# A sum of two weight blocks formed by an accumulating transfer instead of VectorE, in a hybrid encoder block

## The chip, the core and the metric

The kernel runs on one core of a Trainium2 chip. The core's engines work side by side, each through its own list of instructions in order: TensorE (PE) multiplies matrices, VectorE (DVE) and ScalarE (ACT) work element by element on tiles of 128 partitions, GpSimd (POOL) does a little arithmetic and issues transfers, and SyncE (SP) issues transfers only. Transfers between main memory and the core's on-chip memory (SBUF) are carried out by 16 DMA engines, whichever engine issued them. The metric is the device time of one execution, in microseconds; the time before is the median of three runs.

## What is computed

One residual layer over 512 tokens of 2048 features, in float32. Cut to what the change touches:

```python
proj = u @ W_in                        # u = RMSNorm(h); q, k, v, conv_a, conv_b, gates ga and gb
m    = sigmoid(ga) * y_A + sigmoid(gb) * y_B
h    = h + RMSNorm(m @ W_out)
u    = RMSNorm(h)
gate, up = split(u @ W_gate_up)        # 2048 x (2 * 5632)
h    = h + RMSNorm((silu(gate) * up) @ W_down)
```

The two products of the change are those of the gates (two times 2048 output features) and of the FFN's gate and up (two times 5632). All other parts (attention, convolution, output and down projection) keep their code.

## The kernel before

**Layout.** Activations are kept as [feature, token], so weights are the stationary operand and 512 tokens the moving one. A float32 operand is split into a high part (hi, made by a cast on ScalarE, L218 and L124) and a low part (lo, the difference, made on VectorE, L220 and L125); a product is three matmuls, hi by lo, hi by hi and lo by hi (L223 to L225).

**Stages in order.** Convolution inputs, v, q and k with attention, gates, LayerNorm and output projections, FFN gate and up, FFN down projection. The gates' tiles 0 and 1 and the FFN's tiles 0 to 4 run as plain products while the operands of the rest are made. The rest goes in pairs of output tiles through `strassen` (L195): pairs g2 to g15 in the loop at L526 (14 pairs, one tile of ga with one of gb) and pairs f5 to f43 in the loop at L708 (39 pairs, one tile of gate with one of up).

**One pair.** The pair's weights are four quarters of 128 x 1024 float32, 512 KB each: A11 and A12 are the halves of the first tile's rows of weights, A21 and A22 those of the second's. `quarter` (L203) loads each one on SP's queue into a buffer of the pool `wp`, tag `raw`, of which there are six, shared with all other weight loads. `wsum` (L208) makes a sum or difference of two such tiles on VectorE into the pool `stp`, tag `S`, three buffers:

```python
s1 = wsum(a21, a22, ALU.add, 1)
s2 = wsum(s1, a11, ALU.subtract, 2)
s3 = wsum(a11, a21, ALU.subtract, 3)
s4 = wsum(a12, s2, ALU.subtract, 4)
```

`product` (L216) splits one of these weight tiles (three buffers each for hi and lo) and multiplies it by one prepared block of the activations, in 24 matmuls of 128 x 128 by 128 x 256. There are seven products to a pair, in the order A11, S2, S1, S3, A12, S4, A22. A21 has no product of its own. The results go to PSUM tiles x, y and z; VectorE and ScalarE form sums of them in tiles of tag `quad` (L232, L236, L240, L243, L244). Behind each pair the gates' loop applies a sigmoid and stores the result by ScalarE's queue (ga at L531 to L534, gb at L535 to L538), and the FFN's loop forms silu(gate) * up and stores it (L715 to L721).

**What sets the order.** The program is written pair by pair, but the order in which an engine sees its instructions is set by a scheduler, which moves the preparation of the next pair (loads, casts, sums) into the current one as far as buffers allow. The order is then fixed, and each engine waits in it for its next instruction's inputs and buffers. A few loads are pinned to their place in the program (`load_in_order`, L85).

**Other buffers.** The pool `sp` has 69 slots of 128 x 512 float32 (`slot`). In the gates' stage it holds 64 tiles of prepared activation blocks, the column sum of the convolution (csum) and the tiles of ga and gb; in the FFN's stage it holds 56 operand tiles beside those of the results. The down projection reads the FFN's results back from main memory by GpSimd's queue (`load`, tile ad, L705).

Of the kernel before, what the change touches and what calls it, by code (L numbers as in the profile page):

```python
"""Bidirectional hybrid encoder block on one Trainium2 core.

Everything is kept feature-major ([feature, token]), so that a projection is
weights (stationary) times activations (moving, 512 tokens) and the output of
one projection is the moving operand of the next. Tokens are in the order
(column block of 16, grid row, column in block), so that a query block needs
only its own and its neighbouring blocks of keys.

float32 products: each operand is split exactly into hi (12 significant bits)
and lo (the rest, 12 bits), and hi*hi + hi*lo + lo*hi is accumulated in float32.  # L10

Gates and FFN gate/up (but for a few tiles that run while the operands are made)
take one step of Strassen-Winograd on top: their moving operand is RMS-normalized
by token, so that sums of its blocks keep float32's accuracy for every token.
"""
# [10 lines left out]
F32 = mybir.dt.float32  # L26
F32R = mybir.dt.float32r
AF = mybir.ActivationFunctionType
ALU = mybir.AluOpType
AX = mybir.AxisListType  # L30

P = 128
# [17 lines left out]
# where the next part's operands are prepared, in tiles; taps of the convolution per chunk of weights  # L50
# [12 lines left out]
def hybrid_block(ctx: ExitStack, tc, xT, vecs, rpb, mask, w_c0, w_qk, w_v, w_cg, w_ao, w_co, w_out, w_g0, w_gu, w_dn, outT):  # L63
    nc = tc.nc
    PSUM = bass.MemoryType.PSUM
    const = ctx.enter_context(tc.tile_pool(name="const", bufs=1))
    wp = ctx.enter_context(tc.tile_pool(name="wp", bufs=3))
    sp = ctx.enter_context(tc.tile_pool(name="sp", bufs=69))
# [16 lines left out]
    def load_in_order(out, src):  # L85
        """a load behind the loads above it, so that it takes no buffer long before its use"""
        tc.keep_in_program_order(nc.sync.dma_start(out, src))
# [13 lines left out]
    # TensorE's clock is up before the first products  # L101
# [4 lines left out]
    behind = [nc.scalar, nc.tensor]  # L106

    def follow(eng, ins):
        """pins the first instruction of an engine behind what was issued to it before the loads arrive"""
        if eng in behind:  # L110
            behind.remove(eng)
            tc.keep_in_program_order(ins)
# [16 lines left out]
    def split(src, name, scale=None):  # L129
        """src * scale (by partition) as hi + lo"""  # L130
        hi = slot(f"{name}h", F32R)
        lo = slot(f"{name}l", F32R)
        if scale is None:
            nc.scalar.copy(hi, src)
            nc.vector.tensor_tensor(out=lo, in0=src, in1=hi.bitcast(F32), op=ALU.subtract)
        else:
            follow(nc.scalar, nc.scalar.activation(hi, src, AF.Copy, scale=scale))
            nc.vector.scalar_tensor_tensor(
                out=lo, in0=src, scalar=scale, in1=hi.bitcast(F32), op0=ALU.mult, op1=ALU.subtract
            )  # L140
        return hi, lo

    def gemm(outs, acts, name, n=None, more=None, cols=slice(0, NT), between=(), pin=False):
        """ps[128 features, 512 tokens] = src[128, K/128 * 128].T @ acts for each (ps, src) of outs"""
        n = n or len(acts)
        between = iter(between)
        for c in range(0, n, 8):
            w = min(8, n - c)
            while len(acts) < c + w:
                acts.append(more(len(acts)))  # L150
            for i, (ps, src) in enumerate(outs):
                hi, lo = wchunk(src[:, c * P : (c + w) * P], f"{name}_{i}_{c}")
                for k in range(w):
                    s = slice(k * P, (k + 1) * P)
                    ah, al = (t[:, cols] for t in acts[c + k])
                    first, last = c + k == 0, c + k == n - 1
                    mmul = nc.tensor.matmul(ps, hi[:, s], al, start=first, stop=False)  # L157
                    if pin and k == 0:
                        tc.keep_in_program_order(mmul)
                    nc.tensor.matmul(ps, hi[:, s], ah, start=False, stop=False)  # L160
                    nc.tensor.matmul(ps, lo[:, s], ah, start=False, stop=last)  # L161
                next(between, lambda: None)()

    def interleaved(ps, hi, lo, acts, c, cols=slice(0, NT)):
        """the products of two tiles of features (2c, 2c + 1), with the weights for each of the four outputs ps"""
        for k in range(2):
            ah, al = (t[:, cols] for t in acts[2 * c + k])
            for n, o in enumerate(ps):
                o, s = o[:, cols], slice((k * 4 + n) * P, (k * 4 + n + 1) * P)
                first, last = c + k == 0 and cols.start == 0, 2 * c + k == KT - 1  # L170
                follow(
                    nc.tensor, nc.tensor.matmul(o, hi[:, s], ah, start=first, stop=False, skip_group_check=True)
                )
                nc.tensor.matmul(o, lo[:, s], ah, start=False, stop=False, skip_group_check=True)
                nc.tensor.matmul(o, hi[:, s], al, start=False, stop=last, skip_group_check=True)

    def winograd_t(u1, u2, t12, t34):
        """[T1 | T2] and [T3 | T4] of the block columns u1 = [B11 | B12] and u2 = [B21 | B22] (T4 negated)"""
# [16 lines left out]
    def strassen(w0, w1, op, name, n):  # L195
        """
        [w0; w1] (weights of two tiles of outputs, each [128, 2048]) times [B11 B12; B21 B22] by one step of
        Strassen-Winograd: 7 products of half the features by half the tokens in place of 8.
        Returns (C11, P1, C12 = z + u2, C21 = y + P1, C22): C11, z, y in PSUM, the others in SBUF.
        """  # L200
# [25 lines left out]

        a11, a21, a22, a12 = quarter(w0, 0), quarter(w1, 0), quarter(w1, 1), quarter(w0, 1)
        product(x, a11, "11", first=True)
        s1 = wsum(a21, a22, ALU.add, 1)
# [5 lines left out]
        u2 = quad(2)  # L235
# [9 lines left out]
        s4 = wsum(a12, s2, ALU.subtract, 4)  # L245
# [4 lines left out]
    def rstd(acc, n, name, blocks=range(NB), pin=False):  # L250
        """
        1/sqrt(mean + eps) by token (of the given blocks) from tiles [feature, token] whose sum by column
        is that of the squares: [token, block]
        """
# [15 lines left out]
    def by_column(r, name, blocks=range(NB), pin=False):  # L270
        """r [token, block] as a row on all partitions, in PSUM"""
# [14 lines left out]
    def halves(row, acc, name, n, pin=False):  # L286
        """the two steps to 1/rms for half n of the tokens, to row"""
        blocks, cols = range(n * NB // 2, (n + 1) * NB // 2), (A, B)[n]
        r = []
# [5 lines left out]
    def sumsq(acc, x, name, last=False, eng=nc.vector):  # L295
        """acc, a list of tiles, with x*x added (the last one as a tile of its own)"""
# [13 lines left out]
    # x * gain is split; 1/rms, a factor by token, is applied to what is projected from it.  # L310
# [32 lines left out]
    def taps(n):  # L343
        """the next n taps of the convolution, behind what VectorE does for the products"""
# [37 lines left out]
    def normalize(c):  # L382
        """tiles 2c and 2c + 1 of u = RMSNorm_pre(x), split"""
# [218 lines left out]
    # the last two by halves of the tokens, so that 1/rms of the first half is there when the products end  # L602
# [17 lines left out]
    # Gate and up for the first three tiles of the FFN, from h2 * gain: the 1/rms of h2 is applied to the result.  # L620
# [3 lines left out]
    def h2(i, cols):  # L624
        """h2 = x + f * gain / rms(f) into f[i], and its split, for some of the tokens"""
# [36 lines left out]
    # The next two from the normalized u, whose blocks (half of the features, half of the tokens) are kept:  # L662
    # B11 and B12 as [hi | lo] by block, B21 and B22 as hi and lo over all tokens.
# [36 lines left out]
    # The rest by Strassen-Winograd.  # L700
# [46 lines left out]
    # The last two tiles by halves of the tokens, so that the first half is finished beside the second's products.  # L747
# [53 lines left out]
def _mask():  # L801
    """0 where a key column lies in a query column's window, else a number that exp sends to 0"""
# [12 lines left out]
def _layout(x, mix_pre_g, mix_post_g, w_in, rpb, w_attn_o, w_dw, b_dw, conv_ln_g, conv_ln_b, w_conv_o, w_out,  # L815
# [16 lines left out]
    # bias of a query (row r, column c of its block) with a key (row, column of the block before, its own, the next)  # L832
# [5 lines left out]
    # gate and up columns of tiles 0 and 1, 3 and 4 of the FFN, by row of 128  # L838
    gu = w_gate_up[0].reshape(KT // 2, 2, P, 2, FT, P)[:, :, :, :, (0, 1, 3, 4)].reshape(KT // 2, 2, P, 2, 2, 2, P)
    gu = gu.transpose(4, 0, 2, 1, 5, 3, 6).reshape(2, KT // 2, P, 8 * P)  # L840
    # columns a and b of tiles 0 and 1 of the convolution, by row of 128
# [38 lines left out]
```

## Time and profile before

| | us |
|---|---|
| median of three runs | 2603.82 (2601.86 to 2605.2) |
| span of the profiled execution | 2602.3 |
| TensorE busy | 2561.6 |
| VectorE busy | 1748.0 |
| ScalarE busy | 975.4 |
| GpSimd busy | 187.5 |

The profile's page gives no time of its own for the profiled execution beside its span, so the span is taken for it. "Busy" counts the time in which an engine works on an instruction; waiting, and the issuing of transfers, are not in it. A row of the timeline has the start, the duration, the engine, the source line, the operation, the output and the inputs with their shapes, and in brackets how long the engine had been idle and what ended that. Names are those of the tiles, without their running numbers: f18s is any of the sums of pair f18, f18q any of its quarters, f18h and f18l a hi and a lo, f18v a `quad` tile; tiles named g belong to the gates. A releaser such as "PE f L224" names an engine, its output and its line.

### The profile page before, as it was taken

How to read it: one execution, taken by the hardware profiler on the slowest of the kernel's cores; microseconds unless marked ns; L12 is line 12 of the kernel's file. 1: busy time of each engine (PE TensorE's matmuls, PEld its weight loads, DVE VectorE, ACT ScalarE, POOL GpSimd, SP SyncE). 2: the span in 40 equal slices, each digit the busy share in tenths (PEclk: the TensorE clock that was granted, in tenths of full speed). 3: DMA queues.
4: the chain of work that ended last, by engine and by line, in shares of the span. 5: the costliest groups of instructions: out<-in, count | busy, mean ns of one | idle time of the engine just before them, and what ended most of it. 6: DMA issues, size and time to landing. Idle time of an engine off the chain costs nothing.

```text
span 2602.3 us, 38788 instructions
## 1 busy us (share of the span) xinstructions
PE 2561.6 (98%) x15950; PEld 2317.7 (89%) x15950; DVE 1748.0 (67%) x2178; ACT 975.4 (37%) x1351; POOL 187.5 (7%) x207
## 2 busy tenths in 40 slices
PE   9999999999999999998999999999999999999996
PEld 8888888899998888887899999999999988887886
DVE  5999895787775564348988777777777742233336
ACT  5223333444444322224444444444444432233222
POOL 0110222000000020004000000000000010010003
PEclk9999999999999999999999999999999999999998
DMA  6244323233336345233333333333333453353334
GB/s 214 93 130 149 108 93 105 93 130 136 133 122 219 126 146 174 97 119 141 110 118 110 118 126 121 112 117 122 123 119 118 149 197 99 97 170 95 94 92 141
DMA packets 109410, 330.18 MB, mean 127 GB/s; under 512 B 12592, under 2 KB 19888, under 8 KB 109232
## 3 DMA queue, kind: packets, MB, share of 16 engines
q1 hardware_dynamic: 88832, 283.68, 32.6%
q10 hardware_dynamic: 14976, 26.19, 2.7%
q0 software_dynamic: 5424, 17.83, 2.0%
q8 instruction: 125, 2.05, 0.3%
q14 instruction: 53, 0.43, 0.1%
HBM read 295.14 MB, written 32.51 MB: 126 GB/s over the span
## 4 chain that ended last, share of the span: by engine, by line
PE 81%; issue 15%; DVE 3%; DMA 1%; ACT 0%; POOL 0%; DVEq 0%; POOLq 0%; ACTq 0%
PE f L224 10%; PE f L223 10%; PE f L225 10%; PE pd L157 6%; PE pd L160 6%; PE pd L161 5%; PE po L157 2%; PE po L160 2%; PE po L161 2%; PE qk L161 2%; PE qk L160 2%; PE qk L157 2%; PE py L161 2%; PE py L160 2%; PE py L157 2%
## 5 line engine op out<-in xcount | busy, mean ns | idle before, releaser
L125 DVE TENSOR_TENSOR wlo_wd<-raw_wd,whi_wd 128x1024 fp32r<-128x1024 f32 (+1 forms) x90 | 102.3, 1136 | 279.8 <-ACT whi_wd L124 279.4
L124 ACT CAST whi_wd<-raw_wd 128x1024 fp32r<-128x1024 f32 (+1 forms) x90 | 88.4, 982 | 306.8 <-PE pd L160 305.7
L349 DVE SCALAR_TENSOR_TENSOR cv<-z,vec,cv 128x497 f32<-128x497 f32 (+14 forms) x240 | 190.8, 796 | 4.7
L125 DVE TENSOR_TENSOR wlo_wo<-raw_wo,whi_wo 128x1024 fp32r<-128x1024 f32 x36 | 47.5, 1318 | 106.9 <-ACT whi_wo L124 106.9
L705 POOL DMA_DIRECT2D ad<-a_d x44 | 23.7, 541 | 1020.9 <-DVE f36s L210 668.1
L124 ACT CAST whi_wo<-raw_wo 128x1024 fp32r<-128x1024 f32 x36 | 37.9, 1053 | 130.0 <-PE po L160 122.7
L124 ACT CAST whi_y<-raw_y 128x1024 fp32r<-128x1024 f32 x32 | 33.4, 1051 | 81.8 <-PE py L160 74.5
L124 ACT CAST whi_qk<-raw_qk 128x1024 fp32r<-128x1024 f32 x32 | 33.6, 1051 | 77.2 <-PE qk L160 48.0
L125 DVE TENSOR_TENSOR wlo_qk<-raw_qk,whi_qk 128x1024 fp32r<-128x1024 f32 x32 | 40.6, 1269 | 32.0 <-ACT whi_qk L124 31.7
L125 DVE TENSOR_TENSOR wlo_y<-raw_y,whi_y 128x1024 fp32r<-128x1024 f32 x32 | 53.3, 1667 | 10.0 <-ACT whi_y L124 9.8
L578 DVE TENSOR_TENSOR gg<-py,gg 128x512 f32<-128x512 f32 x32 | 22.0, 690 | 55.2 <-PE py L161 55.0
L157 PE MATMUL py<-ycl,whi_y 128*128 128x512 f32 x128 | 49.8, 389 | 0.0
L160 PE MATMUL py<-ych,whi_y 128*128 128x512 f32 x128 | 49.8, 389 | 0.0
L161 PE MATMUL py<-ych,wlo_y 128*128 128x512 f32 x128 | 49.8, 389 | 0.0
L428 POOL TENSOR_TENSOR bm<-braw,msk 128x128 f32<-128x128 f32 x56 | 43.7, 814 | 13.2 <-DMA braw<-in_rpb 13.2
L267 POOL TENSOR_TENSOR r_r<-r_v,mhalf 128x2 f32<-128x2 f32 (+1 forms) x6 | 8.6, 1436 | 465.5 <-DVE r_v L265 465.5
L125 DVE TENSOR_TENSOR wlo_f<-raw_f,whi_f 128x1024 fp32r<-128x1024 f32 x20 | 26.4, 1326 | 6.6 <-ACT whi_f L124 6.6
L457 ACT ACTIVATE sc<-sc,st 128x256 f32<-128x256 f32 (+1 forms) x32 | 18.0, 563 | 33.0 <-DVE st L456 32.0
L124 ACT CAST whi_ca<-raw_ca 128x1024 fp32r<-128x1024 f32 x12 | 12.6, 1053 | 47.2 <-PE cb L160 19.0
L588 POOL TENSOR_TENSOR gg<-gg,gg 128x512 f32<-128x512 f32 x16 | 20.6, 1288 | 113.8 <-ACT whi_y L124 76.5
L157 PEld LDWEIGHTS py<-ycl,whi_y 128*128 128x128 f32 x128 | 24.0, 188 | 5.0
L160 PEld LDWEIGHTS py<-ych,whi_y 128*128 128x128 f32 x128 | 24.0, 188 | 5.0
(11200 smaller groups left out, 10207.1 us busy)
## 6 DMA issues: line engine op xcount, KB each, us to landing
raw_wd<-in_w_dn SPq DMA_DIRECT2D x60, 512.0 KB, 3.5
raw_wo<-in_w_out SPq DMA_DIRECT2D x36, 512.0 KB, 3.6
raw_qk<-in_w_qk SPq DMA_DIRECT2D x32, 512.0 KB, 3.6
raw_wd<-in_w_dn SPq DMA_DIRECT2D x30, 384.0 KB, 3.1
a_d<-sg ACTq DMA_DIRECT2D x44, 256.0 KB, 2.0
ad<-a_d POOLq DMA_DIRECT2D x44, 256.0 KB, 5.0
raw_v<-in_w_v SPq DMA_DIRECT2D x16, 512.0 KB, 4.2
raw_y<-in_w_ao SPq DMA_DIRECT2D x16, 512.0 KB, 3.6
```

What stands on the lines that cost most here:

```text
L124: nc.scalar.copy(hi[:, s], raw[:, s])
L125: nc.vector.tensor_tensor(out=lo[:, s], in0=raw[:, s], in1=hi[:, s].bitcast(F32), op=ALU.subtract)
L157: mmul = nc.tensor.matmul(ps, hi[:, s], al, start=first, stop=False)
L160: nc.tensor.matmul(ps, hi[:, s], ah, start=False, stop=False)
L161: nc.tensor.matmul(ps, lo[:, s], ah, start=False, stop=last)
L223: nc.tensor.matmul(ps, hi[:, s], al, start=first and k == 0, stop=False, skip_group_check=True)
L224: nc.tensor.matmul(ps, hi[:, s], ah, start=False, stop=False, skip_group_check=True)
L225: nc.tensor.matmul(ps, lo[:, s], ah, start=False, stop=last and k == HT - 1, skip_group_check=True)
L349: nc.vector.scalar_tensor_tensor(out=a[:, to], in0=z[:, fr], scalar=col(C_WDW, i * CW + w), in1=a[:, to], op0=ALU.mult, op1=ALU.add)
L428: nc.gpsimd.tensor_tensor(out=bm[:, o + i - i0], in0=raw[:, :, i * BC : (i + 1) * BC], in1=msk[:, o + i - i0, None, :].broadcast_to([P, RO ...
L578: nc.vector.tensor_tensor(out=g, in0=ps, in1=g, op=ALU.mult)
L705: nc.gpsimd.dma_start(t, a_d[k])
```

## The change

In each pair the sum S1 = A21 + A22 is formed in a tile of its own, tag `S1` of the pool `stp`, with two buffers: SP loads A21 into it, and GpSimd then issues a transfer of A22 that adds to what is there. VectorE's addition is left out. A21 and A22 are still loaded as quarters too, for S3 and for the seventh product. S4 is written over S2 in S2's tile. The pool `sp` has 66 slots in place of 69. The rest of the diff blanks comments and docstrings; behind the new lines (L228 to L230), lines are numbered 3 higher than before within `strassen` (L243 is L246) and 4 higher after it (L535 is L539).

```diff
-    sp = ctx.enter_context(tc.tile_pool(name="sp", bufs=69))
+    sp = ctx.enter_context(tc.tile_pool(name="sp", bufs=66))
...
+        s1 = stp.tile([P, 1024], F32, tag="S1", name=f"{name}s1", bufs=2)
+        nc.sync.dma_start(s1, w1[:, :1024])
+        nc.gpsimd.dma_start(s1, w1[:, 1024:], accum_op=ALU.add)
         a11, a21, a22, a12 = quarter(w0, 0), quarter(w1, 0), quarter(w1, 1), quarter(w0, 1)
         product(x, a11, "11", first=True)
-        s1 = wsum(a21, a22, ALU.add, 1)
         s2 = wsum(s1, a11, ALU.subtract, 2)
...
-        s4 = wsum(a12, s2, ALU.subtract, 4)
+        s4 = s2
+        nc.vector.tensor_tensor(out=s4, in0=a12, in1=s2, op=ALU.subtract)
         product(z, s4, "22", last=True)
         product(y, a22, "T4", last=True)
```

The first place is VectorE's list within pair f18, before the change (here a tile's name has its number: s1 to s4 are the sums, v the `quad` tiles, q a quarter, h and l a hi and a lo):

```order
L220 TENSOR_TENSOR f18l_14566<-f18s1_14530,f18h_14564 128x1024
L210 TENSOR_TENSOR f18s4_14657<-f18q_14500,f18s2_14532 128x1024
L210 TENSOR_TENSOR f19s1_14763<-f19q_14729,f19q_14731 128x1024
L220 TENSOR_TENSOR f18l_14598<-f18s3_14594,f18h_14596 128x1024
L236 TENSOR_TENSOR f18v2_14592<-f18_1_14492,f18v1_14534 128x256
L210 TENSOR_TENSOR f19s2_14765<-f19s1_14763,f19q_14727 128x1024
L220 TENSOR_TENSOR f18l_14628<-f18q_14500,f18h_14626 128x1024
L220 TENSOR_TENSOR f18l_14661<-f18s4_14657,f18h_14659 128x1024
L210 TENSOR_TENSOR f19s3_14827<-f19q_14727,f19q_14729 128x1024
L243 TENSOR_TENSOR f18v4_14654<-f18_1_14492,f18v1_14534 128x256
L244 TENSOR_TENSOR f18v4_14654<-f18v4_14654,f18v3_14624 128x256
L220 TENSOR_TENSOR f18l_14689<-f18q_14498,f18h_14687 128x1024
```

S1 and S2 of pair f19 are made in pair f18. The same list of the changed kernel, from S4 of pair f18 to the lo of A22, the last row:

```order
L249 TENSOR_TENSOR f18s2_14533<-f18q_14503,f18s2_14533 128x1024
L722 TENSOR_TENSOR su17_14483<-f17_1_14259,f17v1_14302 128x256
L220 TENSOR_TENSOR f18l_14567<-f18s1_14494,f18h_14565 128x1024
L723 TENSOR_TENSOR sg17_14482<-sg17_14482,su17_14483 128x256
L220 TENSOR_TENSOR f18l_14599<-f18s3_14595,f18h_14597 128x1024
L239 TENSOR_TENSOR f18v2_14593<-f18_1_14492,f18v1_14535 128x256
L210 TENSOR_TENSOR f19s3_14828<-f19q_14730,f19q_14732 128x1024
L220 TENSOR_TENSOR f18l_14629<-f18q_14503,f18h_14627 128x1024
L220 TENSOR_TENSOR f18l_14661<-f18s2_14533,f18h_14659 128x1024
L210 TENSOR_TENSOR f20s2_14999<-f20s1_14960,f20q_14963 128x1024
L246 TENSOR_TENSOR f18v4_14655<-f18_1_14492,f18v1_14535 128x256
L220 TENSOR_TENSOR f18l_14689<-f18q_14501,f18h_14687 128x1024
```

No sum S1 is left, S4 of f18 stands ahead of the lo of its S1, and the S2 that is made within pair f18 is now that of f20, two pairs on, which reads the tile that the transfers of f20 have filled. Between it and the lo of A22 stands one addition.

The second place is ScalarE's list in the gates, at the end of pair g10 and the start of g11, before:

```order
L218 CAST g11h_6543<-g11q_6535 128x1024
L531 ACTIVATE ga10_6522<-g10_0_6298 128x256
L535 ACTIVATE gb10_6523<-g10v4_6461 128x256
L218 CAST g11h_6577<-g11s2_6573 128x1024
L533 ACTIVATE ga10_6522<-ga10_6522 128x256
L534 DMA g_d_4041<-ga10_6522 128x512
L218 CAST g11h_6605<-g11s1_6571 128x1024
L537 ACTIVATE gb10_6523<-gb10_6523 128x256
L538 DMA g_d_4041<-gb10_6523 128x512
L218 CAST g11h_6637<-g11s3_6635 128x1024
```

And the same list of the changed kernel:

```order
L218 CAST g11h_6546<-g11q_6538 128x1024
L535 ACTIVATE ga10_6522<-g10_0_6298 128x256
L218 CAST g11h_6578<-g11s2_6574 128x1024
L537 ACTIVATE ga10_6522<-ga10_6522 128x256
L538 DMA g_d_4041<-ga10_6522 128x512
L218 CAST g11h_6606<-g11s1_6535 128x1024
L539 ACTIVATE gb10_6523<-g10v4_6462 128x256
L541 ACTIVATE gb10_6523<-gb10_6523 128x256
L542 DMA g_d_4041<-gb10_6523 128x512
L218 CAST g11h_6638<-g11s3_6636 128x1024
```

The first sigmoid of gb10 (L535 before, L539 now) has moved behind the store of ga10 and behind the cast of S1.

The third place is SP's list, the issues of weight loads around pair f20, in the changed kernel:

```order
L205 DMA f19q_14736<-in_w_gu 128x1024
L229 DMA f20s1_14960<-in_w_gu 128x1024
L205 DMA f20q_14963<-in_w_gu 128x1024
L205 DMA f20q_14965<-in_w_gu 128x1024
L205 DMA f20q_14967<-in_w_gu 128x1024
L205 DMA f20q_14969<-in_w_gu 128x1024
L229 DMA f21s1_15193<-in_w_gu 128x1024
```

The load of A21 into f20s1 stands ahead of the pair's four quarters; the accumulating transfers of pairs f7 to f43 stand in GpSimd's list one behind the other, that of f43 ahead of the first load of ad.

## Prediction

> **What bounds the kernel now.** Read first the page: the span, the busy line, the slices, the queue of the weight loads and the chain of work that ended last.
>
> ```profile
> span 2602.3 us, 38788 instructions
> PE 2561.6 (98%) x15950; PEld 2317.7 (89%) x15950; DVE 1748.0 (67%) x2178; ACT 975.4 (37%) x1351; POOL 187.5 (7%) x207
> PE   9999999999999999998999999999999999999996
> q1 hardware_dynamic: 88832, 283.68, 32.6%
> PE 81%; issue 15%; DVE 3%; DMA 1%; ACT 0%; POOL 0%; DVEq 0%; POOLq 0%; ACTq 0%
> ```
>
> TensorE (PE) is busy 98% of the span and carries the chain; it idles 2602.3 - 2561.6 = 40.7 us in all. Where, and does VectorE (DVE) cause it where the change takes work from it? Busy time by stretch, inside the gates' pairs, inside the FFN's pairs, and at the end:
>
> ```profile
> core 0: us, PE busy (x) PEld busy (x) DVE busy (x) ACT busy (x) POOL busy (x), PEclk, DMA share, GB/s
> 600.00:800.00 200.00, 200.00 (x1669) 200.00 (x1668) 150.09 (x160) 91.96 (x133) 0.00 (x0) 1.00 0.39 136
> 1440.00:1460.16 20.16, 20.16 (x170) 20.16 (x170) 15.85 (x18) 8.49 (x12) 0.00 (x0) 1.00 0.34 123
> 1600.00:1800.00 200.00, 200.00 (x1669) 200.00 (x1668) 157.80 (x180) 83.64 (x109) 0.00 (x0) 1.00 0.34 117
> 2400.00:2602.00 202.00, 179.03 (x922) 153.97 (x920) 83.11 (x108) 53.67 (x68) 20.67 (x22) 0.95 0.36 110
> ```
>
> In both Strassen stages TensorE has no idle time at the full granted clock (1.00). A stretch of 20.16 us is one pair: 7 products of 24 matmuls, one per 0.12 us. VectorE works 15.85 of the 20.16 us, GpSimd (POOL) not at all. Of the 40.7 idle us, 202.00 - 179.03 = 23 lie in the last stretch, where no pair is computed. So the pairs have no stall that a faster VectorE could remove.
>
> **What the change removes.** One weight sum per pair; for pair f20 the first row holds two of its sums (A21 + A22, and A11 - A21, both of two raw quarters), the second the landing times of its quarters, 512 KB each:
>
> ```profile
> L210 DVE TENSOR_TENSOR f20s<-f20q x2: 1225/1226/1226, 1587.6 to 1594.9; 128x1024 f32<-128x1024 f32 x2
> DMA to landing us min/median/max: 3.5/3.8/4.1
> ```
>
> 14 pairs of gates and 39 of the FFN make 53 sums of 1.226 us: 65 us of VectorE's 1748. All of it lies beside a TensorE that is 100% busy, so on the path it is worth **0**. Forming S4 in S2's tile removes no instruction.
>
> **What it adds: a chain with a deadline.** Per pair one 512 KB load of A21 on SP's queue and one accumulating 512 KB transfer of A22 from GpSimd, into a tile of two buffers. The order of the changed kernel puts S2(n+2), which reads that tile, into pair n, ahead of the last lo, that of A22(n), which TensorE's seventh product needs. VectorE works in order: if the accumulate of pair n+2 is late, the lo of pair n is late and TensorE stalls, in each pair. The chain starts when lo of S1(n) frees the buffer: load, accumulate, S2(n+2), add to C22, lo of A22(n). I work it out for pair f18.
>
> ```profile
> 1563.08 0.42 DVE L720 TENSOR_TENSOR sg<-sg,f17v 128x256 f32<-128x256 f32 x1
> 1563.86 0.42 DVE L718 TENSOR_TENSOR su<-f,f17v 128x256 f32<-128x256 f32 x1 [0.36 <-PE f L225]
> ...
> 1564.87 1.23 DVE L220 TENSOR_TENSOR f18l<-f18s,f18h 128x1024 fp32r<-128x1024 f32 x1
> ...
> 1575.90 0.41 DVE L243 TENSOR_TENSOR f18v<-f,f18v 128x256 f32<-128x256 f32 x1
> 1576.77 1.22 DVE L220 TENSOR_TENSOR f18l<-f18q,f18h 128x1024 fp32r<-128x1024 f32 x1
> ...
> 1581.18 0.28 PE L225 MATMUL f<-t348h,f18l 128*128 128x256 f32 x1
> ```
>
> Start: the lo of S1(18) runs from 1564.87 now. In the new order S4 (1.23 us) stands ahead of it, behind the multiply that ends at 1563.50, then the addition su (0.42): 1563.50 + 1.23 + 0.42 = 1565.15, so the lo ends at about 1566.4 and the load lands 3.8 later, at 1570.2. Deadline: the first matmul that reads the lo of A22(18) is at 1581.18 (the last row); before it come that lo (1.22), one C22 addition (0.41) and S2(20) (1.22), so the accumulate must have landed by 1578.3. **Budget in the FFN: 8.1 us** from its issue to its landing.
>
> In the gates the change also shortens the pool of slots, 69 to 66. 64 operand tiles and csum stay in it there, so one slot is left where four were, and gb takes the slot of ga only when ga's store has landed. On ScalarE (ACT) gb's first sigmoid (L535) moves behind the next cast, and the gb addition on VectorE (L536) with it. The second row below is for ga's stores:
>
> ```profile
> 710.14 0.33 ACTq L534 DMA_DIRECT2D g_d<-ga  x1
> ...
> DMA to landing us min/median/max: 2.7/3.0/4.4
> ...
> 712.52 0.41 ACT L537 ACTIVATE gb<-gb 128x256 f32<-128x256 f32 x1
> ...
> 712.65 1.22 DVE L220 TENSOR_TENSOR g11l<-g11s,g11h 128x1024 fp32r<-128x1024 f32 x1 [0.54 <-ACT g11h L218]
> 723.70 0.42 DVE L243 TENSOR_TENSOR g11v<-g,g11v 128x256 f32<-128x256 f32 x1
> 724.22 0.43 DVE L244 TENSOR_TENSOR g11v<-g11v,g11v 128x256 f32<-128x256 f32 x1
> ...
> 717.49 0.28 PE L225 MATMUL g<-t120h,g11l 128*128 128x256 f32 x1
> 729.01 0.28 PE L225 MATMUL g<-t340h,g11l 128*128 128x256 f32 x1
> ...
> g13q<-in_w_cg SPq DMA_DIRECT2D x4, 512.0 KB, 3.9
> ```
>
> The store lands at 710.14 + 3.0 = 713.1; a sigmoid (0.41) and the addition (0.42) on, at about 714.1 with the waits between engines, the lo of S1(11) can start, instead of 712.65, and end at 715.3. TensorE reads it first at 717.49: 2 us of cover, so the slots by themselves cost **0** (without that cover, up to 1.4 us x 12). But the chain starts later: the load (3.9) lands at 719.2. The deadline is 729.01 - 1.22 - 0.43 - 0.42 - 1.22 = 725.7 (both C22 additions stand there). **Budget in the gates: 6.5 us.** It binds in 12 pairs (g2 to g13 prefetch for g4 to g15), the FFN's in 37 (f5 to f41).
>
> **The price of the accumulate.** No row of before shows one. The nearest rows are GpSimd's loads of ad, 256 KB each:
>
> ```profile
> 1930.47 0.64 POOL L705 DMA_DIRECT2D ad<-a_d  x1 [668.11 <-DVE f36s L210]
> ...
> L705 POOL DMA_DIRECT2D ad<-a_d x44: 537/537/637, 1930.5 to 2339.1; - x44
> ...
> ad<-a_d POOLq DMA_DIRECT2D x1, 256.0 KB, 2.9
> ...
> DMA to landing us min/median/max: 2.7/5.0/7.9
> ```
>
> The one issued within an FFN pair landed in 2.9 us. Bandwidth from the queue's row above: 283.68 MB took 32.6% of 2602.3 us, so 0.524 MB take 1.57 us of all 16 engines. Estimate: 2.9, plus 0.79 for the second 256 KB, plus 1.57 if the destination is read too, plus 0.79 for sharing with the pair's own quarters, which are in flight then (half of one's 1.57): **X = 6.0 us**, below both budgets. Bounds: 2.9 (that row), and 10.0 as two medians of all ad loads (5.0 each, most issued in a row in the down stage). Nearest in size, stage and queue is the first row, so I take 6.0.
>
> The Trainium skill, "Collectives: The Full Stack", on why ReduceScatter has half of AllGather's bandwidth, says that an add in the DMA engine needs two source reads and gives 62.28 against 32.35 GB/s. No run here shows it yet; with that factor of 1.93 the 1.57 us of one such transfer become 3.03, and the sum would be X = 2.9 + 0.79 + 1.46 + 0.79 = 5.9 instead of 6.0.
>
> **What else moves.** Weight traffic in pairs rises from 2 to 3 MB: with the DMA share at 0.34 to 0.39 there, half more is about 0.6, no bound. At the FFN's end the ad loads stand behind the last accumulates on GpSimd's queue:
>
> ```profile
> 2056.43 0.55 POOL L705 DMA_DIRECT2D ad<-a_d  x1 [7.01 <-DVE fa1l L135]
> ...
> 2074.49 0.61 ACT L134 CAST fa4h<-ad 128x512 fp32r<-128x512 f32 x1
> ...
> PE pd L157 <- DVE fa11l L135: 0.3, 1, 0.3
> ```
>
> ad4 is issued at 2056.43 and used at 2074.49; with the later slots I have it issued at about 2068.5, plus 5.0 still before its use. TensorE waited 0.3 us there in all. I count **+1, give or take 2**, for such places together. The sum: 2602.3 + 0 + 0 + 1 = 2603.3 against the profiled execution; the median of the runs shown, 2603.82, stands 1.5 above that span, so about **2605**.
>
> **Rivals.**
> - *Only the gates stall.* X between the budgets, 6.5 to 8.1: (X - 6.5) x 12, at most 1.6 x 12 = 19, so 2605 to 2624; 2616 at 7.4. For it: the budget stands only 0.5 above my X. Against: the 2.9 row.
> - *The accumulate is late everywhere (the slower side).* From X = 8.1 each FFN pair pays (X - 8.1) too: at 9.0, 0.9 x 37 + 2.5 x 12 = 63, so 2668; at 10.0, 1.9 x 37 + 3.5 x 12 = 112, so 2717. For it: the 5.0 and 7.9 of other ad loads, and an unseen kind of transfer. Against: those were queued behind each other.
> - *GpSimd's issue is held up by VectorE.* A hold of one or two sums (1.2 to 2.4 us) makes X 7.2 to 8.4: 0.7 x 12 = 8 to 1.9 x 12 + 0.3 x 37 = 34 us, 2613 to 2639, so its time falls into the two cases above. Against it: the issue of 0.64 us at 1930.47, in a pair in which VectorE is as busy as in the others, against a median of 0.54.
> - *Faster.* VectorE has 65 us more to itself; but with 200.00 of 200.00 us busy on TensorE there is nothing to win in the pairs. At most a few us at the transitions: 2598.
>
> The Trainium skill, "SBUF — State Buffer", describes that third rival as a trap: VectorE's fast modes hold the port that GpSimd needs to write descriptors. The 0.64 us of that one issue gives it little weight here.
>
> **How the numbers follow.** The chances: hidden everywhere 0.45 (2605, its own range 2599 to 2610); only the gates stall 0.22; late everywhere 0.28 (the hold by VectorE is inside these two); faster 0.05. 0.2%, 5.2 us, is about what a measurement of this kernel can tell from no change; a quarter of the second case lies below it. So same 0.45 + 0.05 = 0.50, slower 0.17 + 0.28 = 0.45, faster 0.05. The range takes the bounds of X: from 2599 to 2717 at X = 10.0; left out are the faster case and X beyond 10 (0.1).
>
> **What would show it.** The tile s1's accumulate, from issue to landing: 6 us or less by the forecast. TensorE's busy time in 600 to 800 and 1600 to 1800: 200.00 if hidden; else a wait of TensorE for the lo of the A22 product (L225 for L220) once per pair, the same length in each, with VectorE in turn waiting for the accumulate at S2. VectorE's busy sum down by 65 us in any case. That the 53 sums are gone and 53 loads and 53 accumulates stand in their place is plain from the program's order, so a change without effect is no case of its own. The forecast is wrong if the accumulate lands later than 6.5 us from its issue, if SP's load of A21 starts later than the lo of S1 two pairs back, or if TensorE's clock falls in the pairs.

## The result, and the profile after

The changed kernel takes **2731.7 us**, median of four runs, against 2603.31 for the kernel before, also by four: a ratio of 1.0483, 95% interval 1.047 to 1.0495. It is 128 us slower; the prediction was 2605, with a range up to 2717. The page after (span, busy times, granted clock by slice, the queue of GpSimd's transfers, the chain):

```profile
span 2730.5 us, 38868 instructions
PE 2613.4 (96%) x15950; PEld 2353.0 (86%) x15950; DVE 1657.8 (61%) x2125; ACT 983.0 (36%) x1351; POOL 231.5 (8%) x260
PEclk9999999988999999999999999999999999999998
q0 software_dynamic: 13056, 45.62, 7.3%
PE 56%; DMA 22%; DVE 13%; issue 6%; ACT 1%; POOL 1%; DVEq 0%; POOLq 0%; ACTq 0%
```

VectorE is busy 90 us less (1748.0 to 1657.8). The 53 sums are 65 of these; the other 25 are no work saved, since busy time counts overlapping rows once, and in experiment 3 below it falls to 1728.5 with all 2178 instructions in place. And yet TensorE's share of the chain fell from 81% to 56%, while transfers rose from 1% to 22% and VectorE from 3% to 13%. Something now runs in a circle through VectorE and a transfer. The two Strassen stages, by the same stretches as before:

```profile
core 0: us, PE busy (x) PEld busy (x) DVE busy (x) ACT busy (x) POOL busy (x), PEclk, DMA share, GB/s
600.00:800.00 200.00, 179.14 (x1344) 175.88 (x1344) 108.66 (x119) 74.77 (x104) 6.91 (x8) 0.91 0.54 148
1600.00:1800.00 200.00, 189.40 (x1547) 186.25 (x1547) 129.53 (x160) 78.78 (x101) 7.88 (x9) 1.00 0.58 160
```

TensorE idles in both, where it never did before. Per pair the cost is best read from ScalarE's first cast of one of a pair's sums to that of a later pair; the rows of the kernel before and, behind them, of the changed one (times from first to last start):

```profile
L218 ACT CAST g3h<-g3s x4: 1047/1047/1048, 547.5 to 558.9; 128x1024 fp32r<-128x1024 f32 x4
L218 ACT CAST g15h<-g15s x4: 1047/1047/1049, 789.4 to 800.9; 128x1024 fp32r<-128x1024 f32 x4
...
L218 ACT CAST f6h<-f6s x4: 1047/1048/1053, 1318.9 to 1330.5; 128x1024 fp32r<-128x1024 f32 x4
L218 ACT CAST f43h<-f43s x4: 1047/1048/1051, 2064.9 to 2076.4; 128x1024 fp32r<-128x1024 f32 x4
```

```profile
L218 ACT CAST g3h<-g3s x4: 1045/1046/1047, 546.7 to 564.2; 128x1024 fp32r<-128x1024 f32 x4
L218 ACT CAST g15h<-g15s x4: 1047/1047/1047, 849.8 to 861.3; 128x1024 fp32r<-128x1024 f32 x4
...
L218 ACT CAST f6h<-f6s x4: 1044/1047/1052, 1377.7 to 1395.2; 128x1024 fp32r<-128x1024 f32 x4
L218 ACT CAST f43h<-f43s x4: 1047/1049/1052, 2189.9 to 2201.5; 128x1024 fp32r<-128x1024 f32 x4
```

| | g3 to g15 (12 pairs), us | per pair | f6 to f43 (37 pairs), us | per pair |
|---|---|---|---|---|
| before | 241.9 | 20.16 | 746.0 | 20.16 |
| after | 303.1 | 25.26 | 812.2 | 21.95 |

61.2 us are lost in the gates and 66.2 in the FFN, together 127.4 of the 128.2 by which the span grew. Nothing of note is lost elsewhere.

Where in a pair? First the tile of pair f20's sums: SP's load of A21, GpSimd's accumulate, who waited, and the least and longest landing of the tile's two transfers (the accumulate's is the longest):

```profile
L229 SPq DMA_DIRECT2D f20s<-in_w_gu x1: 327/327/327, 1647.5 to 1647.5; - x1
L230 POOL DMA_DIRECT2D f20s<-in_w_gu x1: 876/876/876, 1652.0 to 1652.0; - x1
...
  DVE f20s L210: 5.4, 1
DMA to landing us min/median/max: 4.0/6.4/8.8
```

The accumulate landed 8.8 us after its issue, at 1660.8, and VectorE sat idle for 5.4 us at S2 for it. Now VectorE's timeline through that pair (start, duration, line, output and inputs; in brackets the idle time ahead and what ended it), and TensorE's first waits behind it:

```profile
1646.23 1.22 DVE L220 TENSOR_TENSOR f18l<-f18s,f18h 128x1024 fp32r<-128x1024 f32 x1
...
1660.83 1.23 DVE L210 TENSOR_TENSOR f20s<-f20s,f20q 128x1024 f32<-128x1024 f32 x1 [5.41 <-DMA f20s<-in_w_gu]
1661.98 0.42 DVE L246 TENSOR_TENSOR f18v<-f,f18v 128x256 f32<-128x256 f32 x1
1662.31 1.22 DVE L220 TENSOR_TENSOR f18l<-f18q,f18h 128x1024 fp32r<-128x1024 f32 x1
1663.44 0.42 DVE L247 TENSOR_TENSOR f18v<-f18v,f18v 128x256 f32<-128x256 f32 x1
1663.78 1.22 DVE L220 TENSOR_TENSOR f19l<-f19q,f19h 128x1024 fp32r<-128x1024 f32 x1
1664.91 0.42 DVE L720 TENSOR_TENSOR sg<-f,f18v 128x256 f32<-128x256 f32 x1
1665.25 1.22 DVE L220 TENSOR_TENSOR f19l<-f19s,f19h 128x1024 fp32r<-128x1024 f32 x1
1666.38 0.42 DVE L724 TENSOR_TENSOR sg<-sg,f18v 128x256 f32<-128x256 f32 x1
1666.71 1.22 DVE L249 TENSOR_TENSOR f19s<-f19q,f19s 128x1024 f32<-128x1024 f32 x1
1667.85 0.42 DVE L722 TENSOR_TENSOR su<-f,f18v 128x256 f32<-128x256 f32 x1
1668.18 1.22 DVE L220 TENSOR_TENSOR f19l<-f19s,f19h 128x1024 fp32r<-128x1024 f32 x1
...
1662.54 0.36 PE L223 MATMUL f<-t348l,f18h 128*128 128x256 f32 x1 [0.76 <-DVE f18v L246]
1663.58 0.38 PE L225 MATMUL f<-t348h,f18l 128*128 128x256 f32 x1 [0.57 <-DVE f18l L220]
```

This is a **ring**. The lo of S1(18) ends at 1647.45 and SP issues the next load at 1647.47. To GpSimd's issue at 1651.98 are 4.5 us, to S2(20) 8.85 more. From there VectorE works without a gap through the 8.6 us of work that piled up behind S2, to the lo of S1(19) at the end of it, and that frees the buffer for the next load, issued at 1669.43. 4.5 + 8.85 + 8.6 = 21.96 us, the time from issue to issue. No product stands on the ring; TensorE waits twice per pair, first for the C22 addition, which has yet to read the tile that the seventh product adds to, then for the lo.

In the gates the ring has a longer last part, from S2 to the lo that frees the buffer. VectorE's rows of pair g10, and the store of ga on ScalarE's queue:

```profile
724.29 1.23 DVE L210 TENSOR_TENSOR g11s<-g11s,g11q 128x1024 f32<-128x1024 f32 x1 [7.06 <-DMA g11s<-in_w_cg]
...
730.15 1.23 DVE L249 TENSOR_TENSOR g10s<-g10q,g10s 128x1024 f32<-128x1024 f32 x1
734.53 0.42 DVE L540 TENSOR_TENSOR gb<-g,g9v 128x256 f32<-128x256 f32 x1 [3.15 <-DMA g_d<-ga]
734.87 1.22 DVE L220 TENSOR_TENSOR g10l<-g10s,g10h 128x1024 fp32r<-128x1024 f32 x1
...
729.47 0.33 ACTq L538 DMA_DIRECT2D g_d<-ga  x1
```

Ahead of the lo of S1(10) VectorE waits 3.15 us for ga's store to land and give its slot to gb. So the circle is 25.6 us here (loads issued at 710.50 and 736.11). No row on it waits for TensorE.

### The profile page after: what moved, and what is told of

Same layout as the page of the kernel before. It is cut to its first block, busy times and chain, and to the rows that moved or that the text cites. A ratio compares the mean times of both kernels' runs of the same rounds, so it can differ in the third digit from the quotient of the medians.

```text
span 2730.5 us, 38868 instructions
## 1 busy us (share of the span) xinstructions
PE 2613.4 (96%) x15950; PEld 2353.0 (86%) x15950; DVE 1657.8 (61%) x2125; ACT 983.0 (36%) x1351; POOL 231.5 (8%) x260
## 4 chain that ended last, share of the span: by engine, by line
PE 56%; DMA 22%; DVE 13%; issue 6%; ACT 1%; POOL 1%; DVEq 0%; POOLq 0%; ACTq 0%
PE pd L157 5%; PE pd L160 5%; PE pd L161 5%; PE po L157 2%; PE po L161 2%; PE po L160 2%; PE qk L161 2%; PE qk L160 2%; PE qk L157 2%; PE py L157 2%; PE py L161 2%; PE py L160 2%; DMA g_d<-ga 2%; PE f L225 2%; PE f L223 2%
## 5 line engine op out<-in xcount | busy, mean ns | idle before, releaser
L582 DVE TENSOR_TENSOR gg<-py,gg 128x512 f32<-128x512 f32 x32 | 22.0, 691 | 55.7 <-PE py L161 55.5
L721 ACT ACTIVATE sg<-sg 128x256 f32<-128x256 f32 x39 | 16.3, 418 | 85.6 <-DVE sg L720 85.5
```

Of the source, the lines that this page charges most:

```text
L582: nc.vector.tensor_tensor(out=g, in0=ps, in1=g, op=ALU.mult)
```

## The experiments

The theory after the result: the ring, with the accumulate's landing and, in the gates, ga's store on it. Its rivals: the third megabyte of loads per pair; the smaller slot pool or S4's place by themselves; GpSimd held up by VectorE.

**1. S2 pinned to its own pair.**

```diff
-        s2 = wsum(s1, a11, ALU.subtract, 2)
+        s2 = stp.tile([P, 1024], F32, tag="S", name=f"{name}s2")
+        tc.keep_in_program_order(nc.vector.tensor_tensor(out=s2, in0=s1, in1=a11, op=ALU.subtract))
```

> The changed kernel with one row moved: S2 of a pair is pinned behind the lo of its own A11, so VectorE forms it in its own pair and not two pairs ahead. Transfers, slots and S4 in S2's tile stay. If the 128 us come from the ring (lo of S1, load, accumulate, S2 two pairs on, lo of the next S1), it is gone: about 2605, TensorE 100% busy in the pairs, the accumulate still 8 to 9 us from issue to landing. If the 3 MB of loads per pair (or the wait of loads for engines) set the time, it stays near 2730. If the short slot pool costs by itself, the gates keep some 1.4 us x 12, so about 2620.

2607.25 us, ratio to before 1.0017 (1.0007 to 1.0026). All transfers are there, and the loss of 128 us is gone but for some 4. The sums' tile of pair f20 in this kernel:

```profile
L230 POOL DMA_DIRECT2D f20s<-in_w_gu x1: 876/876/876, 1574.4 to 1574.4; - x1
L234 DVE TENSOR_TENSOR f20s<-f20s,f20q x1: 1215/1215/1215, 1602.7 to 1602.7; 128x1024 f32<-128x1024 f32 x1
...
DMA to landing us min/median/max: 4.2/6.5/8.8
```

In this pair the accumulate takes the same 8.8 us, and S2 comes 28 us behind its issue, long after the landing. Over all pairs the accumulate is somewhat shorter here than in the changed kernel (on average 7.5 against 8.5 us in the FFN, f7 to f43, and 6.4 against 8.8 in the gates, g4 to g15), so that this experiment alone doesn't clear the latency; the next one does. The traffic, which is all there, is not the cause.

**2. S4 in a tile of its own.**

```diff
-        s4 = s2
-        nc.vector.tensor_tensor(out=s4, in0=a12, in1=s2, op=ALU.subtract)
+        s4 = wsum(a12, s2, ALU.subtract, 4)
```

> The changed kernel with one part undone: S4 has a tile of its own again. VectorE's order then has S2 of pair n+2 one product ahead of the lo of S1(n+1), no longer ahead of the lo of A22(n). Ring theory: load 4.5, accumulate 8.7, S2 1.2, lo of S1 1.2 and some waits make 16 to 17 us per pair, below 20.16, so TensorE isn't held: about 2605 (2603 to 2612). Traffic as the cause: near 2730, as it is unchanged. Accumulate latency alone, whatever the order: near 2730.

2604.29 us, ratio 1.0004 (0.9994 to 1.0014): no difference from before. The stretches, and pair f20's accumulate and S2:

```profile
600.00:800.00 200.00, 200.00 (x1669) 200.00 (x1668) 137.61 (x149) 93.31 (x132) 8.61 (x10) 1.00 0.65 185
1600.00:1800.00 200.00, 200.00 (x1669) 200.00 (x1668) 143.69 (x170) 83.69 (x109) 8.74 (x10) 1.00 0.60 171
...
L230 POOL DMA_DIRECT2D f20s<-in_w_gu x1: 873/873/873, 1571.1 to 1571.1; - x1
L210 DVE TENSOR_TENSOR f20s<-f20s,f20q x1: 1218/1218/1218, 1584.0 to 1584.0; 128x1024 f32<-128x1024 f32 x1
```

With a tile of its own for S4 the scheduler puts S2(20) into pair f19 (12.9 us behind the issue), not into f18. The accumulates land about as late as in the changed kernel (6.8 to 10.3 us, on average 7.9 in the FFN and 8.8 in the gates), at a higher DMA share (0.65 and 0.60), and cost nothing. So neither the traffic nor the latency as such is the cause: the place of S2 in VectorE's queue is. It takes S4's shared tile, and the order that follows from it, to close the ring.

**3. The sum on VectorE again, 66 slots and S4's shared tile kept.**

```diff
-        nc.sync.dma_start(s1, w1[:, :1024])
-        nc.gpsimd.dma_start(s1, w1[:, 1024:], accum_op=ALU.add)
...
+        nc.vector.tensor_tensor(out=s1, in0=a21, in1=a22, op=ALU.add)
```

> The changed kernel with the sum S1 on VectorE again (A21 and A22 from their quarters, no load of A21 into S1's tile, no accumulate); 66 slots and S4 in S2's tile stay. Ring theory: 2603 to 2606, the same as before, since VectorE has 15.85 of 20.16 us to do and no transfer stands between S1 and S2. If the slots or S4's place cost by themselves, the gates are 1.4 us x 12 = 17 longer (2620) or the FFN too (2640 and more).

2605.33 us, ratio 1.0008 (0.9999 to 1.0018). The smaller pool and the shared tile cost nothing measurable while no transfer is on the ring. S2 stands one pair ahead in this kernel; the order with S2 two pairs ahead and a quicker transfer is tried in experiments 4 and 7.

**4. GpSimd's transfer overwrites.**

```diff
-        nc.gpsimd.dma_start(s1, w1[:, 1024:], accum_op=ALU.add)
+        nc.gpsimd.dma_start(s1, w1[:, 1024:])
```

> GpSimd's transfer overwrites in place of adding: S1 is A22 alone, the add is left out; order and traffic from GpSimd's queue stay. If the add is what is slow (reading the destination, 2.77 against 1.57 us of all engines' time and a latency of its own), the transfer lands in 4 to 5 us, the FFN has no stall and the gates little: 2605 to 2640. If GpSimd's queue or the sharing with the quarters is slow, it lands in about 7.5 us: FFN pairs of 20.7, gates of 24, so about 2670.

2646.06 us (one run). Between the two forecasts: in the FFN the first held, in the gates the second. GpSimd's transfers in the changed kernel, in this one and, for the fifth experiment, with two quarters less (pair f23; size, us to landing):

```profile
f23s<-in_w_gu POOLq DMA_DIRECT2D x1, 512.0 KB, 9.4
```

```profile
f23s<-in_w_gu POOLq DMA_DIRECT2D x1, 512.0 KB, 4.4
```

```profile
f23s<-in_w_gu POOLq DMA_DIRECT2D x1, 512.0 KB, 5.5
```

In 1600 to 1800 us the plain transfers land in 4.0 to 5.0 us (f20 to f29), the accumulates of the changed kernel in 7.8 to 9.4 (f18 to f26). The FFN's pairs are back at 20.28 us, so leaving out the add removes nearly all of the FFN's loss. It also shows that GpSimd's queue is not held up by VectorE's work: 512 KB from the same queue beside the same work come in 4.4. In the gates it lands in 5.0 to 7.6 (g4 to g15), and pairs still take 23.37.

**5. Two quarters less.** S3 is A11 - A12 and the seventh product takes A12; A21 and A22 are loaded only for S1.

```diff
-        a11, a21, a22, a12 = quarter(w0, 0), quarter(w1, 0), quarter(w1, 1), quarter(w0, 1)
+        a11, a12 = quarter(w0, 0), quarter(w0, 1)
...
-        s3 = wsum(a11, a21, ALU.subtract, 3)
+        s3 = wsum(a11, a12, ALU.subtract, 3)
...
-        product(y, a22, "T4", last=True)
+        product(y, a12, "T4", last=True)
```

> The changed kernel without the separate loads of A21 and A22: S3 is formed of A11 and A12, and the seventh product takes A12, so two quarters, one load and one accumulate per pair, 2 MB as before the change. If sharing with the quarters in flight makes the accumulate 8.7 us long, it falls to 5.4 to 6 us (what the ones at the ends of the stages took, with little beside them), the FFN has no stall, the gates less: about 2640. If the accumulate is that long by itself, it stays at 8 to 9 and the time near 2730.

2629.07 us (one run), near the first forecast's 2640. The accumulate falls to 5.3 to 7.1 us in both stages, mostly 5.5, as the last row above has it. The FFN's pairs are at 20.18, the gates' at 22.28. So of the accumulate's 8.5 us (the mean of f7 to f43 in the changed kernel) some 3 go with the two quarters that are left out. Whether it is their number, or that they are loads of the same two blocks of weights, this run doesn't tell.

**6. ga's store off the ring.** The store of ga is left out, and gb is stored to both places behind gb's last sigmoid.

```diff
-        nc.scalar.dma_start(g_d[i], ga)
...
         nc.scalar.dma_start(g_d[KT + i], gb)
+        nc.scalar.dma_start(g_d[i], gb)
```

> The changed kernel with the store of ga left out and gb stored into both places behind gb's last sigmoid (the rows of ga in memory are then gb's): as many bytes, same order on VectorE, but gb's slot no longer waits for ga's store to land. If that store stands on the gates' ring, a gates pair shortens from 25.2 us to load 4.5 + accumulate 8.9 + 8.7 of VectorE's queue = 22.1, so 12 x 3.1 = 37 less than the changed kernel: about 2695. If the store is hidden, as the prediction had it, about 2731. FFN pairs stay at 21.9 in both.

2706.18 us, ratio 1.0394 (1.0348 to 1.044), against 2695 expected with the store on the ring. VectorE's rows ahead of the lo of S1(9) now have no wait at gb:

```profile
685.98 1.23 DVE L249 TENSOR_TENSOR g9s<-g9q,g9s 128x1024 f32<-128x1024 f32 x1
687.12 0.41 DVE L539 TENSOR_TENSOR gb<-g,g8v 128x256 f32<-128x256 f32 x1
687.46 1.22 DVE L220 TENSOR_TENSOR g9l<-g9s,g9h 128x1024 fp32r<-128x1024 f32 x1
```

By pairs the forecast holds: the gates' pairs fall from 25.26 to 22.39 us (22.1 expected), the FFN's stay at 21.78. What the whole has more lies behind the gates: from g15's first such cast to f6's are 541.3 us, against 527.9 in the changed kernel. One wait of TensorE there, of 7.3 us for VectorE's multiplication by a gate that is read back (L582), is not in the changed kernel's trace, and experiment 7 has it too (7.5 us). So the edit costs time outside the pairs; why is open.

**7. The same, with the overwriting transfer.** The edits of 4 and 6 together.

> The same, and GpSimd's transfer overwrites in place of adding (the add is left out). If the accumulate's latency and the store's landing are all that the change costs, nothing is left: load 4.5 + transfer 4.2 to 6.8 + 8.7 is at most 20.0, so pairs of 20.16 us in both stages and about 2605 (to 2612). If something else in the changed kernel costs in the gates (its traffic, its slots in another way), about 2646, as with the overwriting transfer alone.

2627.87 us, ratio 1.0093 (1.007 to 1.0116). Pairs take 20.62 us in the gates and 20.22 in the FFN: of the 61.2 and 66.2 us lost in the pairs, 5.5 and 2 are left. The transfers of g11 and g13 still landed in 7.6 and 8.4 us, later than the 6.8 that was reckoned with. The total misses the 2605 because of what lies behind the gates, as in 6: 544.4 us from g15 to f6, 15 more than before's 529.5.

The pairs of all runs in one table, from the same casts (us per pair):

| | S2's place | add | ga's store in the way | gates | FFN |
|---|---|---|---|---|---|
| before | one pair ahead | VectorE | no | 20.16 | 20.16 |
| changed | two ahead | transfer | yes | 25.26 | 21.95 |
| 1, S2 pinned | own pair | transfer | yes | 20.18 | 20.16 |
| 2, S4's own tile | one ahead | transfer | yes | 20.22 | 20.16 |
| 3, VectorE's sum | one ahead | VectorE | yes | 20.16 | 20.16 |
| 4, overwriting | two ahead | none | yes | 23.37 | 20.28 |
| 5, two quarters less | two ahead | transfer | yes | 22.28 | 20.18 |
| 6, gb stored twice | two ahead | transfer | no | 22.39 | 21.78 |
| 7, 4 and 6 | two ahead | none | no | 20.62 | 20.22 |

The ring's sum can be set against this table: 4.5 for the load, the mean landing of the run, 8.6 of VectorE's work, and 3.15 more, as in pair g10, where ga's store is in the way. In the changed kernel that is 25.1 in the gates and 21.6 in the FFN, in experiment 4's gates 22.8, in 5's 21.9, in 6 21.4 and 21.3; the measured pairs are 0.2 to 1.0 us longer. In the FFN of 4, 5 and 7 the sum is 17.7 to 18.7, less than TensorE's 20.16 us of work, and the pairs are back at 20.18 to 20.28. Only 7's gates, with a sum of 19.1 and pairs of 20.62, stay longer than both.

## Why the prediction was wrong

**Right: the removed work is worth nothing.** VectorE makes 53 sums less, 65 us by their rows, and TensorE gained nothing from it; experiments 1 and 2, which keep that gain and break the ring, are at 2607.25 and 2604.29. (That busy time would fall by just 65 us was a wrong sign to look for, as it fell by 90.) The +1 for places outside the pairs held too: on balance 0.8 of the span's 128.2 lie there.

**Right: where it would hurt.** The chain named (lo of S1, load, accumulate, S2 two pairs on, ahead of the lo of A22) is the one that decides, in both stages, and the second rival, the accumulate late everywhere, is what happened. It was given 0.28.

**Wrong: the accumulate's price, X = 6.0.** On average it was 8.5 in the FFN (6.3 to 10.0, f7 to f43) and 8.8 in the gates (7.1 to 9.9, g4 to g15). The nearest row was a plain load of ad, and three additions to it were to make up for the rest. The part that the engines' time covers was not too small: GpSimd's queue took 7.3% of 2730.5 us with the add and 5.4% of 2644.3 without, 56.5 us for 53 transfers, 1.07 each where 1.57 was put. What the sum lacked was latency: in the company of four quarters the add delays the landing by about 4 us (in the FFN a median of 8.4 against 4.3 in experiment 4). With two of them it lands in 5.5, some 1.2 later than the plain one beside four; a plain one beside two was not run.

The Trainium skill, "Collectives: The Full Stack", has 1.93 for an add by its two reads. By the queue's shares here, less before's 2.0% of 2602.3 for its other transfers, an accumulate took 2.78 us of all engines' time in the changed kernel and a plain one 1.71, a factor of 1.62. In the other runs with the add it took 2.7 to 3.1, most in experiment 5 (8.3% of 2627.1), a factor of 1.6 to 1.8. So the measured factor is below the page's, and neither says much of the landing, which doubled.

**Wrong: the budgets, and the price of going over them.** At the measured means the prediction's own formula gives (8.5 - 8.1) x 37 + (8.8 - 6.5) x 12 = 42 us, not 128. Two steps failed.
- It took the ring to close through TensorE, with the next lo of S1 at its old distance from the seventh product. It closes on VectorE: what waits behind S2 runs one after another, 8.6 us, where the formula left 20.16 - 3.8 - 8.1 = 8.3; and from the load's issue to GpSimd's are 4.5 us, not 3.8, since GpSimd starts 0.5 behind the landing. With f20's 8.85 for X, 0.7 + 0.75 + 0.3 make 1.75 of the 1.8 us by which f20's ring is longer than 20.16.
- It put the slots at 0 by themselves, by a cover of 2 us, and let the wait for ga's store count only as a chain that starts 1.4 us later. That cover was TensorE's, for a lo of S1 in time. On the ring the wait (3.15 us in pair g10, where the store lands in 4.9 us and not 3.0) counts in full: experiment 6 takes 2.9 us per pair away. With S2 pinned (experiment 1) it costs nothing, as the prediction had it.

So the range's upper end, 2717 at X = 10, was too low for what a mean X of 8.5 and 8.8 already costs.

**The third rival** (GpSimd held up by VectorE) falls: GpSimd's issue took 0.86 to 0.92 us for every accumulate but that of g3 (1.25, right behind two other issues), and the plain transfer, beside the same work in the FFN, landed in 4.3 (the median). The trap that the Trainium skill's "SBUF — State Buffer" describes is not seen in these runs; VectorE's rows in the pairs are all tensor_tensor, so they say nothing of other operations.

**What stays open**: whether the add's extra landing time beside the quarters is spent waiting in the DMA engines' queues or in slower reads of the destination. No run separates these. Open too is why the plain transfer lands later in the gates (5.0 to 7.6 in experiment 4) than in most of the FFN.

## What to carry to other kernels

Moving work off an engine that isn't the bound gained nothing here, and what it lost was set by where the replacement's consumer stands in an in-order queue. Follow such a chain around until it comes back to the buffer that starts it. If it closes once per iteration and its sum of latencies is longer than the busiest engine's work, that sum is the iteration's length, and every cover that was counted against the old bound is gone. A harmless saving in buffers (here S4 in S2's tile) can change the scheduler's order and close such a ring, so compare the order row by row, and keep a consumer of a slow transfer out of the way until it is needed.

## What the hardware showed that was not expected

- In the FFN's pairs an accumulating transfer of 512 KB from GpSimd landed 5.5 us after its issue with two quarters per pair beside it, 8.4 with four, the plain one 4.3 beside four (medians). The add's own time on the DMA engines is but 1.07 us in the changed kernel (1.0 to 1.4 over all runs with the add).
- GpSimd's issue of the accumulate took 0.88 us, of the plain transfer of the same size 0.54.
- TensorE's granted clock in 600 to 800 us was 0.91 in the changed kernel, where it waits in every pair, and 1.00 in experiment 2. Behind a wait of TensorE its products start every 0.21 us from 727.95 to 733.5, before that wait and from then on every 0.12. So part of the stage's loss shows as busy time: 1344 products of 0.12 us would fill 161 us, and TensorE is busy for 179.14. Its products are not on the ring, and in experiment 5 the gates' pairs take 22.28 us at a clock of 0.99, so the lower clock is taken for a consequence; no run tried it by itself.
